# HGRN2 value projection by seven half-size products instead of eight, moved ahead of attention, its values kept in DRAM

## The chip, the cores and the metric

One core of one Trainium2 chip runs the whole program. The metric is the device time of one execution in microseconds (us). A time of a kernel is the median of several runs; the trace is one further execution taken by the hardware profiler. The engines are TensorE (PE, with its weight loads as PEld), VectorE (DVE), ScalarE (ACT), GpSimd (POOL) and SyncE (SP), whose queue issues nearly all DMA transfers in this kernel.

## What is computed

A hybrid decoder layer on 512 tokens of width 2048. One projection of the normalised input feeds an attention group (16 heads, with compressed, selected and windowed keys and values) and an HGRN2 group (8 heads with a 128x128 state each). Cut to what matters here:

```python
h = rmsnorm(x, norm_in[l])                       # 512 x 2048
proj = h @ w_in[l]
(q_a, k_cmp, v_cmp, k_slc, v_slc, k_win, v_win, gate_a, z_a,
 q_h, f_h, i_h, z_h) = jnp.split(proj, split_at, axis=-1)
o_a = nsa_mixer(q_a, k_cmp, v_cmp, ...)          # attention, 16 heads
o_h = hgrn2_mixer(q_h, f_h, i_h, lbs[l])         # i_h: 512 x 1024, the values of HGRN2
...
x = rmsnorm(x + concat(o_a, o_h, gated) @ w_out[l], final_norm)
```

The change concerns `i_h`, the product of h (512 x 2048) with 1024 columns of `w_in`.

## The kernel before

The normalised input is held transposed in SBUF as 16 tiles `hT[.][k]` of 128 features x 512 tokens, split in two parts: `hh` (rounded to fp32r) and `hl` (the rest). Weights come from DRAM in 512 KB pieces; ACT casts the rounded part (L281) and DVE subtracts for the rest (L282). Each product of a weight tile with an input tile is therefore three matmuls: rounded by rounded, rounded by rest, rest by rounded. A 128x512 matmul is one of those three.

The stages, in the order in which the driver at the end of the program calls them: the input is loaded, squared (ACT L201) and transposed while the compressed keys' projection runs (`first_proj(KC)`, L302 to L304); `x_norm` makes the row scales `rs` and `rs_bc` (DVE L209 and the small operations of `rsqrt`); the compressed values' projection VC (`proj_fm`, L323 to L325, 96 matmuls of 128x512) runs with nothing beside it but the cutting of the key blocks (`blocks(KC)`, SP copies from SBUF to SBUF, DVE L383); then VS (`proj_tm`, L348 to L350, 256 columns) beside the compression of the keys (`compress`, L399), VW and the first queries beside the compression of the values, and attention with further projections between its steps. After attention `hgrn_v(0)` computes four heads' values alone (192 matmuls of 128x512, ACT L832 scales the result by `rs`), and then four pairs of `hgrn_head` run (L730 and others), filled with projections: `hgrn_qf(1)`, `hgrn_v(1)` (192 matmuls more), `hgrn_qf(2)`, `hgrn_qf(3)` and the output gates. `FILL` says how much filling each pair of heads gets. Gates and the output projection end the program.

`run((generator, weight), ...)` interleaves generators by the costs they yield. Each engine carries out its own instructions strictly in one order, which a scheduler fixes at build time, and every DMA issue on SP is such an instruction too: one that waits holds up all those behind it. Buffers come from pools in which a slot is free again when its last reader is done.

## Time and profile before

| what | value |
|---|---|
| median of 3 runs (lowest to highest) | 1105.23 us (1104.85 to 1105.31) |
| the profiled execution: its own time, its span | 1106.74 us, 1104.7 us |
| granted TensorE clock, mean | 0.997 |
| TensorE matmuls busy | 1086.3 us, 98% of the span |
| VectorE, ScalarE, GpSimd busy | 572.0, 394.3, 76.1 us |
| DMA traffic | 109.60 MB, mean 99 GB/s |

The profiled execution is 2.0 us longer than its span (launch and end lie around it) and 1.5 us longer than the median. TensorE's busy time counts overlapping matmuls once; the mean duration of one matmul is longer than the distance between the starts of two, because they are pipelined. In rows of single instructions the time in front is the start from the span's beginning, the next the duration; what stands in brackets is the idle time ahead and what ended it.

### The profile page before, as it was taken

The numbers are of one execution on the slowest core, as the hardware profiler recorded it, in microseconds if no ns is written. First come the engines' busy times: TensorE is split into PE (matmuls) and PEld (weight loads), VectorE is DVE, ScalarE is ACT, GpSimd is POOL, SyncE is SP. The second block draws the span as 40 slices with busy tenths as digits, with TensorE's granted clock in tenths as the row PEclk, the third lists the DMA queues.
The fourth block names the chain that finished last, engine by engine and source line by source line (L and its number), as shares of the span: only waits on it lengthen the run. The fifth ranks groups of instructions, "written<-read, shape, count | busy, mean of one in ns | idle before, by whom it ended". The sixth has DMA issues, their size and how long they took to land.

```text
span 1104.7 us, 15078 instructions
## 1 busy us (share of the span) xinstructions
PE 1086.3 (98%) x5682; PEld 896.8 (81%) x5682; DVE 572.0 (52%) x1438; ACT 394.3 (36%) x798; POOL 76.1 (7%) x134
## 2 busy tenths in 40 slices
...
GB/s 256 122 142 191 115 145 104 71 83 58 115 59 57 76 39 39 96 77 96 77 77 61 92 78 80 82 81 73 76 130 81 95 115 115 126 112 173 96 86 124
DMA packets 91751, 109.60 MB, mean 99 GB/s; under 512 B 5584, under 2 KB 60448, under 8 KB 91680
## 3 DMA queue, kind: packets, MB, share of 16 engines
...
## 4 chain that ended last, share of the span: by engine, by line
PE 94%; DMA 2%; ACT 1%; DVE 1%; issue 1%; SPq 0%; ACTq 0%
PE pj L348 13%; PE pj L349 13%; PE pj L350 13%; PE pj L323 10%; PE pj L325 10%; PE pj L324 10%; PE ot L581 4%; PE pj L562 3%; PE lp L730 3%; DMA w<-in_w_in_dram 2%; PE lp L548 2%; PE lp L549 1%; PE pj L973 1%; PE pj L972 1%; PE pj L974 1%; PE lp L399 1%
## 5 line engine op out<-in xcount | busy, mean ns | idle before, releaser
L282 DVE TENSOR_TENSOR w<-w,w 128x1024 fp32r<-128x1024 f32 (+3 forms) x151 | 182.3, 1208 | 255.7 <-PE pj L349 87.1
L281 ACT CAST w<-w 128x1024 fp32r<-128x1024 f32 (+3 forms) x151 | 156.8, 1039 | 300.1 <-DMA w<-in_w_in_dram 188.7
L348 PE MATMUL pj<-w,hh 128*128 128x512 f32 (+2 forms) x608 | 229.1, 377 | 0.0
L349 PE MATMUL pj<-w,hl 128*128 128x512 f32 (+2 forms) x608 | 225.1, 370 | 0.0
L350 PE MATMUL pj<-w,hh 128*128 128x512 f32 (+2 forms) x608 | 224.5, 370 | 0.0
L323 PE MATMUL pj<-hh,w 128*128 128x512 f32 x480 | 194.8, 406 | 0.0
L325 PE MATMUL pj<-hh,w 128*128 128x512 f32 x480 | 189.1, 394 | 0.0
L324 PE MATMUL pj<-hl,w 128*128 128x512 f32 x480 | 188.9, 393 | 0.0
L350 PEld LDWEIGHTS pj<-w,hh 128*128 128x128 f32 x608 | 114.2, 188 | 18.8
L348 PEld LDWEIGHTS pj<-w,hh 128*128 128x128 f32 x608 | 114.5, 188 | 18.1 <-ACT s L486 0.4
L349 PEld LDWEIGHTS pj<-w,hl 128*128 128x128 f32 x608 | 114.5, 188 | 17.7
L325 PEld LDWEIGHTS pj<-hh,w 128*128 128x128 f32 x480 | 90.2, 188 | 19.4 <-issue 0.9
L324 PEld LDWEIGHTS pj<-hl,w 128*128 128x128 f32 x480 | 90.4, 188 | 16.9 <-issue 0.5
L323 PEld LDWEIGHTS pj<-hh,w 128*128 128x128 f32 x480 | 90.3, 188 | 16.9 <-issue 0.7
L522 ACT ACTIVATE s<-s,mn 128x128 f32<-128x128 f32 (+3 forms) x128 | 71.7, 561 | 41.6 <-DVE mn L517 36.5
L517 DVE CUSTOM_DVE_ANT_0 s<-s,lp 128x128 f32<-128x128 f32 (+3 forms) x128 | 60.3, 483 | 37.2 <-PE lp L549 18.5
L562 PE MATMUL pj<-ident,s 128*128 128x128 f32 x320 | 53.7, 275 | 0.7 <-ACT s L522 0.5
L581 PE MATMUL ot<-pt,s 128*64 128x512 f32 (+3 forms) x256 | 47.9, 441 | 1.4 <-ACT pt L571 1.4
L562 PEld LDWEIGHTS pj<-ident,s 128*128 128x128 f32 x320 | 39.5, 140 | 11.1 <-ACT s L522 4.7
L571 ACT COPY pt<-pj 128x256 f32<-128x256 f32 (+2 forms) x56 | 25.8, 461 | 48.0 <-PE pj L562 47.8
L581 PEld LDWEIGHTS ot<-pt,s 128*64 128x64 f32 x256 | 22.2, 136 | 23.5 <-issue 10.5
L348 PE MATMUL pj<-w,s 128*128 128x512 f32 x96 | 37.5, 391 | 0.0
...
## 6 DMA issues: line engine op xcount, KB each, us to landing
w<-in_w_in_dram SPq DMA_DIRECT2D x115, 512.0 KB, 3.6
w<-in_w_out_dram SPq DMA_DIRECT2D x32, 512.0 KB, 3.8
s<-s SPq DMA_DIRECT2D x56, 128.0 KB, 2.3
s<-in_x_dram SPq DMA_DIRECT2D x16, 256.0 KB, 6.5
l<-in_x_dram SPq DMA_DIRECT2D x12, 256.0 KB, 3.2
out_dram<-l SPq DMA_DIRECT2D x12, 256.0 KB, 2.7
...
w<-in_cmp_w_k_dram SPq DMA_DIRECT2D x4, 512.0 KB, 5.8
```

The source lines that it names most:

```text
L281: nc.scalar.copy(hi, raw)
L282: nc.vector.tensor_tensor(lo, raw, hi.bitcast(FP32), ALU.subtract)
L323: nc.tensor.matmul(acc[j], wh, hh, start=kk == 0, stop=False)
L324: nc.tensor.matmul(acc[j], wh, hl, start=False, stop=False)
L325: nc.tensor.matmul(acc[j], wl, hh, start=False, stop=kk == NK - 1)
L348: nc.tensor.matmul(o, ah, hi[:, k, :], start=kk == 0, stop=False)
L349: nc.tensor.matmul(o, al, hi[:, k, :], start=False, stop=False)
L350: nc.tensor.matmul(o, ah, lo[:, k, :], start=False, stop=kk == NK - 1)
L517: nc.vector.tensor_tensor_reduce(out=y, in0=e["bias"][:, 384 - i * P:512], in1=lp, scale=1.0, scalar=3e38, op0=ALU.add, op1=ALU.min, accum ...
L522: nc.scalar.activation(y, y, AF.Exp, bias=mn, scale=-1.0, accum_out=e["ls"][:, 2 * i + b:2 * i + b + 1])
L562: nc.tensor.transpose(tps[:, j * P:(j + 1) * P], y[:, j * P:(j + 1) * P], ident)
L581: nc.tensor.matmul(e["ot"][b * 64:(b + 1) * 64, j * P:512], v_tok[j][:, b * 256 + g * DH:b * 256 + (g + 1) * DH], e["pt"][:, b, j * 512:38 ...
```

## The change

The values `i_h` are a product of h, cut into 2 x 2 blocks, with the weights, cut into 2 x 2 blocks: eight half-size products before. `seven` computes them by seven products of sums and differences of blocks. With 48 matmuls of 128x512 for a half-size product, 336 matmuls take the place of 384. The blocks of h are called A11, A12, A21, A22 (A21 lies in the second half of the tokens of every even k), their sums S1 to S4; the blocks of the weights are combined while they are loaded (`first`, `second`, `third`), one j for each pair of k tiles, j = 0 to 7.

The new stage stands between VC and VS, with pools of its own (`s2`, `s14`, `u`, `e`) that are closed before the slabs and weight pools of the rest are opened. `second_proj` is the VC projection in eight steps of two k tiles (12 matmuls each); beside it `all_sums` makes S1 to S4 on DVE and ACT, one j a step. S3 is written over A21, which is copied to DRAM beforehand (8 transfers, `a21`) and brought back afterwards (8 transfers). `seven` runs three groups of products: (A11, S2, S3), (A12, A22), (S1, S4), whose results are added up by DVE, scaled by ACT and stored to DRAM (8 transfers of 256 KB, `v_scr`). `rows_back` reads four of them back after attention and four before the second pair of heads. The compressed keys' and values' projections go to DRAM as well (`keep`), and the copies of `blocks` read from there, after the new stage. The masks of attention are made after the new stage too. `hgrn_v` is gone, NLATE and FILL are changed. Rows of the changed kernel's order, below, carry its own line numbers.

```diff
-NLATE = 13
+NLATE = 18
-FILL = (62, 62.5, 62, 41)
+FILL = (51, 46, 45, 45)
+NU = 32
+NE = 10
...
+    def parts(src, shape=None):
+        hi, lo = [t if shape is None else t.rearrange(shape[0], **shape[1]) for t in (u(F32R), u(F32R))]
+        nc.scalar.copy(hi, src)
+        nc.vector.tensor_tensor(lo, src, hi.bitcast(FP32), ALU.subtract)
+        return hi, lo
...
+    def second_proj(acc):
+        acc += [pj(), pj()]
+        for k0 in range(0, NK, 2):
+            hi, lo = parts(load_u(w_in2, k0, C_VC), KC2)
+            for j in range(2):
+                js = slice(j * P, (j + 1) * P)
+                for k in range(2):
+                    hh, hl = hT[0][k0 + k], hT[1][k0 + k]
+                    nc.tensor.matmul(acc[j], hi[:, k, js], hh, start=k0 + k == 0, stop=False)
+                    nc.tensor.matmul(acc[j], hi[:, k, js], hl, start=False, stop=False)
+                    nc.tensor.matmul(acc[j], lo[:, k, js], hh, start=False, stop=k0 + k == NK - 1)
+            yield 2.7
...
+    def corner(q, part):
+        return hb[part][q][:, 0:4:2, 256:512].bitcast(FP32)
+    sums = {}
+    def sums_of(j):
+        (x0, y0), (x1, y1) = [[hT[part][k].bitcast(FP32) for part in range(2)] for k in (2 * j, 2 * j + 1)]
+        a0, a1, t = u(), u(), [u(), u()]
+        nc.vector.tensor_tensor(a0, x0, y0, ALU.add)
+        nc.vector.tensor_tensor(a1, x1, y1, ALU.add)
+        s3, s2, s1, s4 = t[0][:, 0:256], t[0][:, 256:512], t[1][:, 0:256], t[1][:, 256:512]
+        nc.vector.tensor_tensor(s3, a0[:, 256:512], a0[:, 0:256], ALU.subtract)
+        nc.vector.tensor_tensor(s1, a0[:, 256:512], a1[:, 256:512], ALU.add)
+        nc.vector.tensor_tensor(s2, a0[:, 0:256], s1, ALU.subtract)
+        nc.vector.tensor_tensor(s4, a1[:, 0:256], s2, ALU.add)
+        d2 = [space["s2"].tile([P, 256], F32R, name=nm("s2"), tag=f"s2_{part}{j}", bufs=1) for part in range(2)]
+        d14 = [space["s14"].tile([P, 512], F32R, name=nm("s14"), tag=f"s14_{part}{j}", bufs=1) for part in range(2)]
+        d3 = [hT[part][2 * j][:, 256:512] for part in range(2)]
+        sums[j] = {"S2": d2, "S1": [d[:, 0:256] for d in d14], "S4": [d[:, 256:512] for d in d14], "S3": d3,
+                   "A11": [hT[part][2 * j][:, 0:256] for part in range(2)],
+                   "A12": [hT[part][2 * j + 1][:, 0:256] for part in range(2)],
+                   "A22": [hT[part][2 * j + 1][:, 256:512] for part in range(2)]}
+        for (hi, lo), src in ((d2, s2), (d3, s3), (d14, t[1])):
+            nc.scalar.copy(hi, src)
+            nc.vector.tensor_tensor(lo, src, hi.bitcast(FP32), ALU.subtract)
+    def all_sums():
+        for q in range(4):
+            for part in range(2):
+                nc.sync.dma_start(out=a21[part][q], in_=corner(q, part))
+            for j in (2 * q, 2 * q + 1):
+                sums_of(j)
+                yield 2.7
...
+    w_half = w_in2.rearrange("(j h p) c -> h p j c", h=2, p=P)
+    free_banks = [(pj, pj), (pj, pj), (ps_lp, ps_lp), (ps_tp, ps_ot)]
+    def seven(c0, done):
+        def load(h, j, right):
+            raw = u()
+            nc.sync.dma_start(out=raw, in_=w_half[h][:, j, c0 + 512 * right:c0 + 512 * right + 512])
+            return raw
+        def group(products, prepare):
+            banks = [free_banks.pop(0) for _ in products]
+            accs = [[f() for f in b] for b in banks]
+            for j0 in range(0, 8, 2):
+                ops = [prepare(j) for j in (j0, j0 + 1)]
+                for i, name in enumerate(products):
+                    for tt in range(2):
+                        ts = slice(tt * P, (tt + 1) * P)
+                        for j in (j0, j0 + 1):
+                            ah, al = [a[:, ts] for a in sums[j][name]]
+                            hi, lo = ops[j - j0][i]
+                            nc.tensor.matmul(accs[i][tt], ah, hi, start=j == 0, stop=False)
+                            nc.tensor.matmul(accs[i][tt], al, hi, start=False, stop=False)
+                            nc.tensor.matmul(accs[i][tt], ah, lo, start=False, stop=j == 7)
+            free_banks.extend(banks)
+            return accs
+        t2 = [None] * 8
+        def first(j):
+            b22, b12, b11 = load(1, j, 1), load(0, j, 1), load(0, j, 0)
+            nc.vector.tensor_tensor(b12, b12, b22, ALU.subtract)
+            t2[j] = u()
+            nc.vector.tensor_tensor(t2[j], b12, b11, ALU.subtract)
+            return parts(b11), parts(t2[j]), parts(b12)
+        def second(j):
+            b21, t4 = load(1, j, 0), u()
+            nc.vector.tensor_tensor(t4, t2[j], b21, ALU.add)
+            return parts(b21), parts(t4)
+        def third(j):
+            b22 = load(1, j, 1)
+            nc.vector.tensor_tensor(t2[j], t2[j], b22, ALU.add)
+            return parts(t2[j]), parts(b22)
+        add = lambda out, a, b: nc.vector.tensor_tensor(out, a, b, ALU.add)
+        p1, p6, p7 = group(("A11", "S2", "S3"), first)
+        c11, u2, u3, c21 = [[ev(), ev()] for _ in range(4)]
+        for tt in range(2):
+            nc.scalar.copy(c11[tt], p1[tt])
+        for tt in range(2):
+            add(u2[tt], p6[tt], c11[tt])
+        for tt in range(2):
+            add(u3[tt], p7[tt], u2[tt])
+        p2, p4 = group(("A12", "A22"), second)
+        for tt in range(2):
+            add(c11[tt], p2[tt], c11[tt])
+            done(0, tt, c11[tt])
+        for tt in range(2):
+            add(c21[tt], p4[tt], u3[tt])
+            done(0, 2 + tt, c21[tt])
+        p5, p3 = group(("S1", "S4"), third)
+        for tt in range(2):
+            add(u3[tt], p5[tt], u3[tt])
+            add(u2[tt], p5[tt], u2[tt])
+            done(1, 2 + tt, u3[tt])
+        for tt in range(2):
+            add(u2[tt], p3[tt], u2[tt])
+            done(1, tt, u2[tt])
...
+    def v_done(half, t, y):
+        nc.scalar.mul(y, y, rs[:, 0, t:t + 1])
+        nc.sync.dma_start(out=v_scr[half][t], in_=y)
...
+    def keep(acc):
+        fs = [dram(), dram()]
+        for j in range(2):
+            f = ev()
+            nc.vector.tensor_tensor(f, acc[j], rs_bc, ALU.mult)
+            nc.sync.dma_start(out=fs[j], in_=f)
+        return fs
...
-    def hgrn_v(c):
-        hv[c] = [late() for _ in range(NT)]
-        def done(t, acc):
-            nc.scalar.mul(hv[c][t], acc, rs[:, 0, t:t + 1])
-        yield from proj_tm([], w_in2, hT, C_IH + c * 512, 512, done)
+    def rows_back(scr_, alloc):
+        tiles = [alloc() for _ in range(NT)]
+        for t in range(NT):
+            nc.sync.dma_start(out=tiles[t], in_=scr_[t])
+        return tiles
...
-    kblk = blocks(KC, 32)
-    run((proj_fm(VC, C_VC, 256), 1))
+    kf = keep(KC)
+    run((second_proj(VC), 22), (all_sums(), 22))
+    vf = keep(VC)
+    seven(C_IH, v_done)
+    first_part.close()
+    slabs = ctx.enter_context(ExitStack())
+    for name in ("w", "slab"):
+        space[name] = slabs.enter_context(tc.tile_pool(name=name, bufs=1))
+    att = ExitStack()
+    space["att"] = att.enter_context(tc.tile_pool(name="att", bufs=1))
+    for q in range(4):
+        for part in range(2):
+            nc.sync.dma_start(out=corner(q, part), in_=a21[part][q])
+    kblk = blocks(kf, 32)
...
-    run((hgrn_v(0), 41))
+    hv[0] = rows_back(v_scr[0], late)
     sz = [[] for _ in range(4)]
-    fill = chain(hgrn_qf(1), hgrn_v(1), hgrn_qf(2), hgrn_qf(3), z_proj(C_ZA, sz[0]), z_proj(C_ZA + 512, sz[1]))
+    fill = chain(hgrn_qf(1), hgrn_qf(2), hgrn_qf(3), z_proj(C_ZA, sz[0]), z_proj(C_ZA + 512, sz[1]))
     for c, t in enumerate(FILL):
+        if c == 1:
+            hv[1] = rows_back(v_scr[1], late)
```

Where the change moves instructions, at three places. **VectorE during the VC projection.** Before, what stands there is the end of the row scales, the weight subtractions (L282), two multiplications of the KC result from the PSUM tiles `pj` (L367) and the cutting of the key blocks (L383):

```order
L211 TENSOR_SCALAR rs<-rs 128x4 [waits DVE_49]
L282 TENSOR_TENSOR w_577<-w_574,w_576 128x1024 [waits DMAHW2_49,Activation_49]
L367 TENSOR_TENSOR s_502<-pj_191,rs_bc 128x512 [waits DMAHW6_49,Activation_49]
L367 TENSOR_TENSOR s_510<-pj_192,rs_bc 128x512 [waits DMAHW0_49]
L282 TENSOR_TENSOR w_607<-w_604,w_606 128x1024 [waits DMAHW3_49,Activation_49]
L383 TENSOR_TENSOR s_518<-s_504,col 128x4x31 [waits DMAHW5_49,DMAHW4_49]
```

Now one step of `second_proj` with `all_sums` reads as follows (j = 3; `u_641` and `u_642` are the two parts of a VC weight chunk, the `s_` tiles the parts of S2 and of S1 with S4, `hh_28` and `hl_29` the input tiles of a quad, in whose A21 corner S3 is written):

```order
L315 TENSOR_TENSOR u_642<-u_639,u_641 128x512 [waits DMAHW3_49,DMAHW2_49,Activation_49]
L372 TENSOR_TENSOR u_657<-hh_28_148,hl_29_149 128x512 [waits DMAHW5_49]
L373 TENSOR_TENSOR u_658<-hh_28_148,hl_29_149 128x512 [waits DMAHW6_49]
L375 TENSOR_TENSOR u_659<-u_657 128x256 [waits DVE_49]
L376 TENSOR_TENSOR u_660<-u_657,u_658 128x256 [waits DVE_49]
L377 TENSOR_TENSOR u_659<-u_657,u_660 128x256 [waits DVE_49]
L388 TENSOR_TENSOR hl_29_149<-u_659,hh_28_148 128x256 [waits Activation_49]
L378 TENSOR_TENSOR u_660<-u_658,u_659 128x256 [waits DVE_49]
L388 TENSOR_TENSOR s_165_668<-u_659,s_164_667 128x256 [waits Activation_49]
L388 TENSOR_TENSOR s_167_670<-u_660,s_166_669 128x512 [waits Activation_49]
L315 TENSOR_TENSOR u_680<-u_677,u_679 128x512 [waits DMAHW4_49,Activation_49]
```

Eight such steps stand one behind the other, and the last row is the first of the next step: 10 operations a step, of 512 and of 256 columns, and the VC chunk's subtraction (L315) of a step stands behind all the sums of the step before. Three subtractions (L388) wait for casts on ACT. The same 8 steps, with 4 multiplications (L537) and 27 small operations, fill all of DVE's rows from `rs`'s first (L232, before L209) to the first of `seven` (L429).

**SyncE during the first group of products.** The `u_` tiles are weights for `first` (three loads a j); the L1101 rows bring the A21 corner of the first quad back from DRAM, and wait for the products with S3 of j = 0 and 1:

```order
L405 DMA u_925<-in_w_in_dram 128x512 [waits DMAHW0_49,PE_49]
L405 DMA u_927<-in_w_in_dram 128x512 [waits DMAHW1_49]
L405 DMA u_929<-in_w_in_dram 128x512 [waits DMAHW2_49]
L1101 DMA hl_27_147<-d_163 128x2x256 [waits DMAHW3_49,PE_49]
L1101 DMA hh_26_146<-d_159 128x2x256 [waits DMAHW4_49,PE_49]
L405 DMA u_946<-in_w_in_dram 128x512 [waits DMAHW5_49,Activation_49]
L405 DMA u_948<-in_w_in_dram 128x512 [waits DMAHW6_49,DVE_49]
L405 DMA u_950<-in_w_in_dram 128x512 [waits DMAHW7_49,DVE_49]
L405 DMA u_1003<-in_w_in_dram 128x512 [waits DMAHW0_49,DVE_49]
```

Nothing stood here before. The three loads for j = 3 come behind the two returns; the pattern comes again ahead of the loads for j = 5 and for j = 7 and once ahead of the second group's load for j = 1.

**SyncE at the beginning of VS.** Before, VS's first weights (`w_634`, `w_668`) and the first compression weights were issued behind the key block copies while VC ran:

```order
L145 DMA w_634<-in_w_in_dram 128x4x256 [waits DMAHW4_49,Activation_49]
L395 DMA s_688<-in_cmp_w_k_dram 128x2x64 [waits DMAHW5_49]
L395 DMA s_688<-in_cmp_w_k_dram 128x2x64 [waits DMAHW6_49]
L145 DMA w_668<-in_w_in_dram 128x4x256 [waits DMAHW7_49,PE_49]
L390 DMA w_686<-in_cmp_w_k_dram 128x4x256 [waits DMAHW0_49,PE_49,Activation_49]
L390 DMA w_725<-in_cmp_w_k_dram 128x4x256 [waits DMAHW1_49,PE_49]
L145 DMA w_747<-in_w_in_dram 128x4x256 [waits DMAHW2_49,DVE_49,PE_49]
```

Now the stores of the values (L474) stand among the loads. The first row is the last of four stores, ahead of the third group's load for j = 1; then come the store of the third group's first finished product, VS's first weights `w_1688`, three stores, a compression weight, the eight key block reads from DRAM (the first of them shown), and VS's second weights `w_1767`:

```order
L474 DMA d_170<-e_1166 128x512 [waits Activation_49]
L405 DMA u_1396<-in_w_in_dram 128x512 [waits DMAHW7_49,DVE_49,PE_49]
...
L474 DMA d_173<-e_1163 128x512 [waits DMAHW6_49,Activation_49]
L160 DMA w_1688<-in_w_in_dram 128x4x256 [waits DMAHW7_49,PE_49]
L474 DMA d_174<-e_1164 128x512 [waits DMAHW0_49,Activation_49]
L474 DMA d_171<-e_1161 128x512 [waits DMAHW1_49,Activation_49]
L474 DMA d_172<-e_1162 128x512 [waits DMAHW2_49,Activation_49]
L568 DMA w_1706<-in_cmp_w_k_dram 128x4x256 [waits DMAHW3_49]
L547 DMA s_1603<-d_511 64x512 [waits DMAHW4_49,DMAHW2_49,DMAHW5_49,DMAHW1_49,DMAHW6_49,DMAHW0_49,DVE_49]
...
L568 DMA w_1745<-in_cmp_w_k_dram 128x4x256 [waits DMAHW4_49]
L160 DMA w_1767<-in_w_in_dram 128x4x256 [waits DMAHW5_49]
```

VS's first weights now stand behind a store that waits for a finished product of the third group, the key block reads behind the last stores, and VS's second weights behind those reads.

## Rows read from the trace of the kernel before

**Rows 1.** The page, part 1: busy us, share of the span, instructions.

```profile
PE 1086.3 (98%) x5682; PEld 896.8 (81%) x5682; DVE 572.0 (52%) x1438; ACT 394.3 (36%) x798; POOL 76.1 (7%) x134
```

**Rows 2.** The page, part 4: the chain that ended last, by engine.

```profile
PE 94%; DMA 2%; ACT 1%; DVE 1%; issue 1%; SPq 0%; ACTq 0%
```

**Rows 3.** PE by time, end of VC: start us, duration us, instruction.

```profile
61.02 0.39 PE L325 MATMUL pj<-hh,w 128*128 128x512 f32 x1
61.25 0.28 PE L348 MATMUL pj<-w,hh 128*128 128x256 f32 x1
61.37 0.28 PE L349 MATMUL pj<-w,hl 128*128 128x256 f32 x1
```

**Rows 4.** VC's stretch: busy PE, PEld, DVE, ACT, POOL; clock, DMA share, GB/s.

```profile
38.50:61.25 22.75, 22.59 (x101) 18.44 (x101) 13.19 (x44) 5.56 (x7) 0.00 (x0) 1.00 0.67 189
```

**Rows 5.** DVE in order of time, beginning of VC, as in rows 3.

```profile
36.29 0.17 DVE L209 TENSOR_REDUCE ss<-ss_in 128x4 f32<-128x20 f32 x1 [3.91 <-ACT s L201]
...
39.87 0.16 DVE L130 TENSOR_TENSOR rxt<-rxi 128x4 f32<-128x4 f32 x1
...
40.58 0.16 DVE L133 TENSOR_TENSOR rxi<-rxi,rxt 128x4 f32<-128x4 f32 x1
```

**Rows 6.** DVE in order of time, an attention step with 512 columns.

```profile
283.67 0.69 DVE L446 TENSOR_TENSOR s<-s,s 128x512 fp32r<-128x512 f32 x1 [2.54 <-ACT s L445]
284.28 0.55 DVE L517 CUSTOM_DVE_ANT_0 s<-s,lp 128x384 f32<-128x384 f32 x1
```

**Rows 7.** ACT in order of time, the cast ahead of that subtraction.

```profile
283.02 0.61 ACT L445 CAST s<-s 128x512 fp32r<-128x512 f32 x1
```

**Rows 8.** DVE in order of time, 256 columns in an HGRN2 head.

```profile
784.31 0.42 DVE L714 TENSOR_TENSOR s<-s,s 128x256 f32<-128x256 f32 x1
784.64 0.42 DVE L709 TENSOR_TENSOR s<-s,s 128x256 f32<-128x256 f32 x1
```

**Rows 9.** DVE in order of time, PSUM multiplications and block cutting.

```profile
42.31 1.29 DVE L367 TENSOR_TENSOR s<-pj,rs_bc 128x512 f32<-128x512 f32 x2
...
49.82 2.29 DVE L383 TENSOR_TENSOR s<-s,col 128x124 f32<-128x124 f32 x8 [0.52 <-DMA s<-s]
```

**Rows 10.** An issue on SP's queue: start us, duration us, transfer.

```profile
48.96 0.53 SPq L145 DMA_DIRECT2D w<-in_w_in_dram  x1
```

**Rows 11.** DMA issues: transfer, queue, count, KB each, median us to landing.

```profile
w<-in_w_in_dram SPq DMA_DIRECT2D x115, 512.0 KB, 3.6
...
s<-s SPq DMA_DIRECT2D x56, 128.0 KB, 2.3
s<-in_x_dram SPq DMA_DIRECT2D x16, 256.0 KB, 6.5
l<-in_x_dram SPq DMA_DIRECT2D x12, 256.0 KB, 3.2
```

**Rows 12.** The end of the program by stretch, columns as in rows 4.

```profile
1097.00:1098.00 1.00, 0.00 (x0) 0.00 (x0) 0.85 (x5) 0.00 (x0) 0.00 (x0) 0.92 0.00 0
1098.00:1099.00 1.00, 0.00 (x0) 0.00 (x0) 0.94 (x3) 0.78 (x2) 0.00 (x0) 0.50 0.00 0
```

**Rows 13.** PE in order of time, the first work of the program.

```profile
5.81 1.12 PE L192 MATMUL lp<-ident,w 128*128 128x128 f32 x4 [3.04 <-DMA w<-in_x_dram]
...
9.51 0.63 PE L302 MATMUL pj<-hh,w 128*128 128x512 f32 x1
9.94 0.63 PE L303 MATMUL pj<-hl,w 128*128 128x512 f32 x1
...
12.68 0.40 PE L303 MATMUL pj<-hl,w 128*128 128x512 f32 x1
12.92 0.39 PE L304 MATMUL pj<-hh,w 128*128 128x512 f32 x1
```

**Rows 14.** DVE in order of time, preparing the first heads after attention.

```profile
456.40 0.69 DVE L851 TENSOR_TENSOR s<-pj,rs_bc 128x512 f32<-128x512 f32 x1
...
458.74 0.43 DVE L709 TENSOR_TENSOR s<-s,s 128x256 f32<-128x256 f32 x1 [0.19 <-POOL s L745]
```

149 lines of the change are left out of this document (89 added, 60 removed).

## The prediction, made before the change was run

> **What bounds the kernel now.** I read the page's busy line and chain first: TensorE is busy 98% of the span [rows 1] and makes up 94% of the chain that ended last [rows 2]. What TensorE is relieved of is therefore gained, and what it is made to wait for is lost, nearly in full. VectorE's 52% [rows 1] is an average; the change puts its work in one place, so the stage counts. In VC's stretch (38.50 to 61.25) TensorE is busy 22.59 of 22.75 us, VectorE 13.19, ScalarE 5.56 [rows 4]. After it the next matmul, VS's first, follows at 0.23 us, the spacing of VC's own 128x512 matmuls; 256 columns take 0.12 [rows 3]. I price matmuls by these start distances, not by the mean duration (0.39 us in the same rows), which overlaps.
>
> **The change part by part.** The sum is made against the profiled execution's own 1106.7 us, 1.5 above the median.
>
> *A, matmuls removed.* 384 less 336 is 48, by 0.23 us: **-11.0**.
>
> *B, the sums.* Beside VC, VectorE gets ten operations a step where TensorE has 12 matmuls, 12 x 0.23 = 2.8 us. Prices: a 512-column subtraction starts 0.61 us ahead of its successor and lasts 0.69 itself [rows 6]; with 256 columns 0.33 and 0.42 [rows 8]. A step is three 512-column operations (the chunk's subtraction L315 and two additions), 3 x 0.61 = 1.83; four additions of 256 columns, 1.32, plus 0.1 because L377 needs L376's end; two subtractions of 256, 0.66; and the S1/S4 subtraction, 0.61. That last one waits for a cast of 512 columns on ScalarE, 0.61 [rows 7], which can only begin when L378 has ended, 0.42 after its start, and only one 256-column operation lies beside: 0.42 + 0.61 + about 0.08 for the two handovers, less 0.66, is 0.45. Together 5.0 us against TensorE's 2.8. The bounds are 4.4 (starts only, no wait) and 5.7 (durations throughout, with the wait). VectorE begins at 36.3 (its reduction of the squares) and has 8 steps, 40.0; 27 small operations that stay, 0.10 each by the seven starts from 39.87 to 40.58 [rows 5], 2.7; four multiplications out of PSUM at 0.65 [rows 9], 2.6; then the first three operations of the new stage, 1.9. So the third matmul of group 1 starts at 83.5, the two ahead of it 0.46 earlier, at 83.0 where VS began at 61.25: **+21.8** (17 to 27.5). VectorE then waits for no more than that one cast a step; TensorE is the one that waits, before each chunk's third matmul.
>
> *C, returns ahead of loads.* In group 1 the loads of j = 3, 5, 7 are queued on SP behind two returns that wait for the end of the pair before. From there: two returns and two loads issued, 4 x 0.53 [rows 10], the third load (the one whose product comes first) landing 3.2 later (256 KB, [rows 11]), a cast of 0.61: 5.9 us, while TensorE has the 18 matmuls of the even j, 4.1. Three times 1.8: **+5.4**. Bounds: 0 if landing is as quick as the smallest row here (2.3 us, 128 KB) and the returns start a little early, three times 5.1 with the 6.5 us that such a load took in company [rows 11].
>
> *D, group 1 to 2.* The same with one load: 2 x 0.53 + 3.2 + 0.61 = 4.9 against 12 matmuls of j = 0, 2.8: **+2.1** (0 to 5.4).
>
> *E, group 2 to 3.* The load of j = 1 stands behind four stores. From the group's last matmul: four additions on VectorE, 2.4, the last scaling on ScalarE 0.65, the store's issue 0.53, the load 3.2, its addition 0.69, its cast 0.61: 8.1. TensorE has only j = 0 in between, 2.8, which itself begins 3.7 late (the four additions, its own addition and its cast): **+5.3** (3 to 9).
>
> *F, group 3 to VS.* VS's first weights are issued behind the store of the first finished product. That product's last matmul lies 9 matmuls, 2.1 us, ahead of the group's end T; addition 0.69, scaling 0.61, issue 0.53 bring it to T - 0.3; the 512 KB land 3.6 later [rows 11]; the cast, two times 512 columns, 1.2: VS starts at T + 4.5, and its fifth matmul needs the subtraction, 1.2 more, against 0.6 of work ahead: +5.1. Next late are the key blocks: the last store is issued at T + 2.1, the eight reads wait for its landing (about T + 5), 8 x 0.53 of issue, 2.3 to landing, a cut of 2.29 / 8 [rows 9]: T + 11.5, when VS's 48 matmuls (0.12 each) run out at about T + 11. The second compression weight and VS's second weights are issued behind those reads and come 0.5 to 1 us late each: +2. Together **+7.1** (3 to 13). Before, all of this ran under VC. The masks now made by GpSimd ahead of the blocks' last columns end inside this wait.
>
> *G, the clock.* The granted clock is 1.00 in VC's stretch [rows 4]; at the program's end, with no matmul after 1095.2, it is 0.92 in the stretch from 1097 and 0.50 (1.2 GHz) from 1098 [rows 12]. The idle times of E and F (3.7 before group 3 begins, 4.5 before VS) are as long. I put 2 us for slow restarts (0 to 13, below). The Trainium skill, "TensorE: Matmul & The Clock Gate", section "Why this matters for your kernels", warns of gaps between bursts of matmuls, after which the clock is back at half. By that rule the half-idle VC stage and each start of a group would be slow, and the sum would come to the time of the third rival; this trace agrees only as far as its end shows the drop, since no burst follows there.
>
> *H, the heads.* Before, 192 matmuls lie between attention and the first head; now only 13 follow the second head's gate values, 3.0 us. That head's preparation takes 2.8 (456.40 to 459.17, [rows 14]): just covered, **0** (-1 to +4). The reads of V (3.2 us each) go out before the heads and are hidden by their first levels; without that cover they would cost some 3 us, inside these bounds. Smaller fillings take matmuls away from the heads, but no VectorE work is added.
>
> Sum: -11.0 + 21.8 + 5.4 + 2.1 + 5.3 + 7.1 + 2 = +32.7, or 1139.4 for such an execution, 1.5 less for the median: **1138**.
>
> **The rivals.**
> 1. *Only the sums stand in the way.* C to F shrink to their lower ends, about 6 in all, because transfers land earlier on a queue that moves little else. Then 1105.2 - 11.0 + 21.8 + 6 = 1122. For it: a 128 KB transfer lands in 2.3 us. Against: the waits for results, not landings, make most of E and F.
> 2. *Slow restarts.* The stage with gaps drops TensorE to 1.2 GHz. At the program's start matmuls came 0.43 apart (9.51 to 9.94) and 0.24 from 12.68 on [rows 13]; from 5.81 to about 12.4 it worked at the slow rate, so that half of 6.6, 3.3 us, was lost. Four such starts (three groups and VS) cost 13.2, and in VC 12 x 0.43 = 5.2 against 5.0 a step costs 1.6 more; less G's 2: 1151. The granted clock in the records of those stretches would decide.
> 3. *Faster: the sums hide.* If a VectorE step took less than 3.6 us, group 1 would begin less than 11 us late, at 72; with C to F at nothing the whole gains. At 2.8 a step it begins at 36.3 + 22.4 + 2.7 + 2.6 + 1.9 - 0.46 = 65.4, and the time is 1105.2 - 11.0 + 4.2 = 1098. Against it: starts alone give 4.4 a step.
> 4. *No net change*: a step near 3.6, as just said, or heads that gain what the stage loses. No row speaks for either.
>
> **How the numbers follow.** Forecast 0.60, as likely as the ten operations' prices and the order of the queue are sure. Its own range is 1128 to 1150: B's bounds, with half of the widths of C to F. Rival 1 has 0.17 and rival 2 0.17; rival 3 has 0.03 and no net change 0.03. The range that is to hold the time 8 times in 10 reaches over rivals 1 and 2: below, 17 for B and 8 for C to F give 1119; above, rival 2 with some 6 of late landings gives 1157. What a measurement here can tell from no change is 0.2%, 2.2 us: faster 0.03, same 0.03, slower 0.94.
>
> **What would show it.** In the changed kernel's trace: VectorE busy nearly without a break from 36 to 83, with TensorE at about half in that stretch, waiting for VectorE at the VC lines; the first matmul of `seven` near 83; in group 1 three waits of some 2 us for loads, with SP's returns just ahead; some 4 us idle ahead of group 3 and ahead of VS, with stores among the loads; 48 matmuls fewer. A and the heads are right if everything after VS has the same length but for 384 matmuls less. The forecast fails if VectorE's operations overlap more than these rows show, if SP's queue is not what holds the loads, or if the clock falls in the gaps.

## The result, and the profile after

| kernel | median of the runs (lowest to highest) | ratio to before, 95% interval |
|---|---|---|
| before | 1105.04 us (1104.44 to 1105.31) | |
| changed | 1170.45 us (1167.69 to 1171.13) | 1.0588 [1.0570, 1.0606] |

The change costs 65 us. The direction was foreseen, the size was not: 33 were predicted, and the result lies 13 us above the wider range (1119 to 1157). The changed kernel's page, its busy line and its chain by engine (before: [rows 1, 2]):

```profile
PE 1109.2 (95%) x5634; PEld 897.7 (77%) x5634; DVE 649.5 (56%) x1603; ACT 420.9 (36%) x871; POOL 73.6 (6%) x134
PE 86%; DMA 5%; DVE 3%; ACT 2%; SPq 1%; issue 1%; ACTq 0%; DVEq 0%
```

TensorE has 48 instructions fewer, yet is busy 23 us longer: part of the loss is in the matmuls, not in waits. What TensorE waited for (line and tile, releaser: us in total, times, longest):

```profile
PE pj L419 <- ACT u L314: 20.2, 7, 4.1
PE pj L354 <- ACT u L314: 11.7, 7, 2.6
PE pj L520 <- ACT w L307: 5.8, 1, 5.8
...
PE lp L577 <- POOL s L287: 1.6, 1, 1.6
```

The second row is VC beside the sums, the first the seven products, the third VS's first matmul, the fourth the compression of the keys, which waits for the masks. The waits and their causes follow in order of time. VectorE's step of VC goes from one L315 to the next:

```profile
54.71 0.69 DVE L315 TENSOR_TENSOR u<-u,u 128x512 fp32r<-128x512 f32 x1
...
59.09 0.69 DVE L388 TENSOR_TENSOR s<-u,s 128x512 fp32r<-128x512 f32 x1 [0.35 <-ACT s L387]
59.70 0.69 DVE L315 TENSOR_TENSOR u<-u,u 128x512 fp32r<-128x512 f32 x1
```

Then come TensorE at the beginning of group 1, SP's queue and TensorE around the first return, the transition to group 3, and VS's first matmul with the SP rows ahead of it:

```profile
84.41 0.79 PE L419 MATMUL pj<-u,hh 128*128 128x512 f32 x1 [4.11 <-ACT u L314]
85.00 0.63 PE L420 MATMUL pj<-u,hl 128*128 128x512 f32 x1
85.43 0.63 PE L421 MATMUL pj<-u,hh 128*128 128x512 f32 x1
...
95.58 0.59 SPq L1101 DMA_DIRECT2D hl<-d  x1
96.27 0.56 SPq L1101 DMA_DIRECT2D hh<-d  x1
96.92 3.02 SPq L405 DMA_DIRECT2D u<-in_w_in_dram  x6
...
104.10 0.80 PE L419 MATMUL pj<-u,hh 128*128 128x512 f32 x1 [4.12 <-ACT u L314]
...
167.29 0.50 PE L419 MATMUL pj<-u,s 128*128 128x512 f32 x1 [2.27 <-ACT u L314]
171.56 0.50 PE L419 MATMUL pj<-u,s 128*128 128x512 f32 x1 [1.24 <-ACT u L314]
...
190.87 0.33 SPq L474 DMA_DIRECT2D d<-e  x1
191.28 0.39 SPq L160 DMA_DIRECT2D w<-in_w_in_dram  x1
196.77 0.58 PE L520 MATMUL pj<-w,hh 128*128 128x256 f32 x1 [5.83 <-ACT w L307]
```

These are stretches of the new stage (length; busy PE, PEld, DVE, ACT, POOL; then the granted clock, DMA share, GB/s; before: [rows 4]):

```profile
60.00:70.00 10.00, 8.23 (x23) 6.11 (x23) 7.38 (x16) 2.02 (x5) 0.00 (x0) 0.67 0.05 18
70.00:80.00 10.00, 6.46 (x27) 4.53 (x25) 9.00 (x20) 4.00 (x9) 0.00 (x0) 1.00 0.00 0
80.00:90.00 10.00, 5.89 (x15) 4.39 (x14) 8.95 (x17) 4.58 (x9) 0.00 (x0) 0.68 0.73 237
...
120.00:130.00 10.00, 9.83 (x34) 7.48 (x32) 3.75 (x6) 1.47 (x3) 0.00 (x0) 0.77 0.27 81
```

The reader is to see two more things here. First, the granted clock, 1.00 in VC before, drops in VC and after most of the long idle times, and the matmuls of 85.00 and 85.43 start 0.43 apart, at 1.2 GHz. Second, there is a loss that no wait shows. These are the matmuls of one line of the projections by operands (duration min/median/max in ns), two rows of after and one of before:

```profile
L522 PE MATMUL pj<-w,hh x480: 277/394/582, 198.0 to 1114.6; 128*128 128x512 f32 x117, 128*128 128x256 f32 x22, 128*128 128x304 f32 x21
L522 PE MATMUL pj<-w,s x96: 387/389/397, 980.6 to 1092.1; 128*128 128x512 f32 x96
L350 PE MATMUL pj<-w,hh x608: 278/389/529, 61.5 to 1050.6; 128*128 128x512 f32 x120, 128*128 128x256 f32 x16, 128*128 128x304 f32 x16
```

In after, the moving operand of the first row lies in the pool `big` (`hh`), that of the second in a slab tile (`s`): the median is 394 ns against 389. (The rows with `hh` hold some matmuls of 256 and 304 columns too; most have 512, and the median is one of these.) Before, it was 389 for both. The starts say it better. The first two rows are the ends of a run of 14 matmuls at full clock at the end of group 2 of after, 0.234 us apart; the last two are the ends of a run of eight before, 0.227 apart:

```profile
161.58 0.39 PE L420 MATMUL pj<-u,hl 128*128 128x512 f32 x1
164.62 0.40 PE L421 MATMUL pj<-u,hh 128*128 128x512 f32 x1
...
999.84 0.39 PE L348 MATMUL pj<-w,hh 128*128 128x512 f32 x1
1001.43 0.39 PE L349 MATMUL pj<-w,hl 128*128 128x512 f32 x1
```

In group 3 of the same trace, whose two operands lie in `u` and `s14`, the distance is 0.227 again (176.04 to 190.55). In the built kernel before, `big`, which holds the weights too, and the slabs begin at 64 bytes past a multiple of 256. The changed kernel no longer keeps that: `big` is at 64, but `small`, which the allocator has put behind it, moves `u`, `w`, `s2`, `s14` and the slabs to 224. Counted over the two built programs, 16 of the 3472 matmuls of 128x512 before have operands that begin at different places modulo 256; now 2944 of 3424 have, 2928 of them 160 bytes apart.

### The profile page after: what moved, and what is told of

Read it like the earlier page. It is cut to its first block, busy times and chain, and to the rows that moved or that the text cites. A ratio compares the mean times of both kernels' runs of the same rounds, so it can differ in the third digit from the quotient of the medians.

```text
span 1169.4 us, 15419 instructions
## 1 busy us (share of the span) xinstructions
PE 1109.2 (95%) x5634; PEld 897.7 (77%) x5634; DVE 649.5 (56%) x1603; ACT 420.9 (36%) x871; POOL 73.6 (6%) x134
## 4 chain that ended last, share of the span: by engine, by line
PE 86%; DMA 5%; DVE 3%; ACT 2%; SPq 1%; issue 1%; ACTq 0%; DVEq 0%
PE pj L520 10%; PE pj L522 10%; PE pj L521 10%; PE pj L495 9%; PE pj L497 9%; PE pj L496 8%; PE ot L758 4%; PE pj L739 3%; PE lp L907 3%; DMA w<-in_w_in_dram 2%; DMA u<-in_w_in_dram 2%; PE lp L725 2%; PE lp L726 1%; PE pj L1167 1%; PE pj L1168 1%; PE pj L1169 1%
## 5 line engine op out<-in xcount | busy, mean ns | idle before, releaser
L308 DVE TENSOR_TENSOR w<-w,w 128x1024 fp32r<-128x1024 f32 (+1 forms) x126 | 152.8, 1214 | 189.1 <-ACT w L307 62.5
L307 ACT CAST w<-w 128x1024 fp32r<-128x1024 f32 (+1 forms) x126 | 130.9, 1040 | 234.0 <-DMA w<-in_w_in_dram 153.5
L520 PE MATMUL pj<-w,hh 128*128 128x512 f32 (+2 forms) x480 | 181.3, 378 | 5.8 <-ACT w L307 5.8
L495 PE MATMUL pj<-hh,w 128*128 128x512 f32 x448 | 184.8, 413 | 0.0
L497 PE MATMUL pj<-hh,w 128*128 128x512 f32 x448 | 178.4, 398 | 0.0
L521 PE MATMUL pj<-w,hl 128*128 128x512 f32 (+2 forms) x480 | 178.2, 372 | 0.0
L522 PE MATMUL pj<-w,hh 128*128 128x512 f32 (+2 forms) x480 | 177.7, 372 | 0.1
L520 PEld LDWEIGHTS pj<-w,hh 128*128 128x128 f32 x480 | 91.8, 191 | 21.1 <-ACT w L307 6.4
L522 PEld LDWEIGHTS pj<-w,hh 128*128 128x128 f32 x480 | 91.3, 191 | 16.2 <-DVE w L308 0.3
L521 PEld LDWEIGHTS pj<-w,hl 128*128 128x128 f32 x480 | 91.9, 191 | 14.8
L497 PEld LDWEIGHTS pj<-hh,w 128*128 128x128 f32 x448 | 84.2, 188 | 20.2 <-issue 1.0
L495 PEld LDWEIGHTS pj<-hh,w 128*128 128x128 f32 x448 | 84.3, 188 | 16.9 <-issue 0.7
L314 ACT CAST u<-u 128x512 fp32r<-128x512 f32 x72 | 42.1, 619 | 65.1 <-DMA u<-in_w_in_dram 38.4
L315 DVE TENSOR_TENSOR u<-u,u 128x512 fp32r<-128x512 f32 x72 | 47.9, 688 | 14.0 <-ACT u L314 12.6
```

Of the source, the lines that this page charges most:

```text
L307: nc.scalar.copy(hi, raw)
L308: nc.vector.tensor_tensor(lo, raw, hi.bitcast(FP32), ALU.subtract)
L495: nc.tensor.matmul(acc[j], wh, hh, start=kk == 0, stop=False)
L497: nc.tensor.matmul(acc[j], wl, hh, start=False, stop=kk == NK - 1)
L520: nc.tensor.matmul(o, ah, hi[:, k, :], start=kk == 0, stop=False)
L521: nc.tensor.matmul(o, al, hi[:, k, :], start=False, stop=False)
```

## The experiments

Each time is a median in us, followed by its ratio to runs of the kernel before on the same chip (1106.2 to 1106.4 us) with the 95% interval. "After" is the changed kernel. It was timed on another chip, on which the kernel before took 1105.0, so differences of medians to it are uncertain by some 1.3 us.

### Where the operands lie

The theory is that the distance of two matmuls depends on where their operands begin in SBUF. The rival is that the longer distance comes with the new work beside it.

```diff
a_pad    -            a, pre = sm(3, "la"), sm(1, "lp")
         +            a, pre = sm(3, "la"), sm(1, "lp", bufs=1)
b_shift  (the kernel before, the same edit, and a tile ahead of hT)
         +    big.tile([P, 8], FP32, name="pad", tag="pad", bufs=1)
a_align       small = ctx.enter_context(tc.tile_pool(name="small", bufs=2))
         +    big = ctx.enter_context(tc.tile_pool(name="big", bufs=1))
         (big opened behind small, no longer ahead of it)
```

> The changed kernel with 4 bytes a partition fewer in a small pool, so that the pools behind it (s2, w, s14, u, slab) begin 32 bytes earlier, at a multiple of 64 as the input tiles hh and hl do; no instruction differs but one small buffer that is no longer doubled. Theory A (operand placement: a matmul whose two operands differ by 32 modulo 64 bytes starts 7 ns later): the spacing of 128x512 matmuls falls from 0.234 to 0.227 us throughout, and the time from 1170 to about 1152 to 1156. Theory B (the whole chip or the profile was slower, placement does nothing): same time within 2 us, spacing unchanged.

Measured: 1168.6, 1.0562 [1.0542, 1.0582], a miss: a common multiple of 64 is not what counts. The pools move by 32 bytes, so that the operands differ by 128 modulo 256. The same 14 matmuls (161.41 to 164.43) are 0.232 apart, the median duration is 392 ns: between the two others. The time is within the spread of after.

> The kernel before with a 32-byte gap between the weight buffers w and the input tiles hh and hl (slab moves along with hh); nothing else. Theory A (placement): spacing of the weight matmuls goes from 0.227 to 0.234 us, and the time from 1105 to between 1117 and 1129. Theory B: 1105 within 2 us.

Measured: 1122.4, 1.0144 [1.0129, 1.0159]. This is the kernel before with 32 bytes more in front of its input tiles and no other work; it is 16 us slower. The slabs move with the input tiles, the weights do not, so that both of these rows are slow:

```profile
L351 PE MATMUL pj<-w,hh x608: 277/395/532, 61.1 to 1064.4; 128*128 128x512 f32 x120, 128*128 128x256 f32 x16, 128*128 128x304 f32 x16
L351 PE MATMUL pj<-w,s x96: 390/396/399, 928.5 to 1042.0; 128*128 128x512 f32 x96
```

> The changed kernel with the two lines swapped that open the pools big (input tiles) and small, so that every pool read by TensorE begins at the same place modulo 256 bytes as the input tiles (224; in the changed kernel the input tiles lie at 64 and the rest at 224, in the kernel before all at 64); no instruction differs. The 4-byte-fewer run put the difference at 128 modulo 256 and left the spacing at 0.2325. Theory A (a 128x512 matmul starts 6 to 8 ns later unless its operands agree modulo 256): spacing 0.227 throughout, time 1170 less 15 to 20, 1150 to 1156. Theory B (the spacing has another cause): 1168 to 1172.

Measured: 1158.0, 1.0464 [1.0444, 1.0484], 12.4 us less than after (somewhat less than the 15 to 20 expected), with the order of two lines exchanged:

```profile
L522 PE MATMUL pj<-w,hh x480: 278/389/582, 194.8 to 1101.6; 128*128 128x512 f32 x117, 128*128 128x256 f32 x22, 128*128 128x304 f32 x21
```

The theory stands: the distance was 0.227 us at equal remainders modulo 256, 0.232 at a difference of 128, 0.233 to 0.234 at odd multiples of 32. The rival falls with b_shift, which has no new work, and with a_align, which has all of it.

### The returns on SP's queue (step C)

```diff
-            nc.sync.dma_start(out=corner(q, part), in_=a21[part][q])
+            nc.gpsimd.dma_start(out=corner(q, part), in_=a21[part][q])
```

> The changed kernel with the eight returns of the A21 corners issued from GpSimd's queue in place of SP's. Theory A (the loads of j = 3, 5, 7 are late because the returns ahead of them on SP wait for a pair's end): the three waits of 4.1 us in group 1 shrink to under 1 us, with them some slow restarts, and the time falls by 12 to 18 us, to 1152 to 1158. Theory B (the loads wait for buffer slots or for the DMA engines): the waits stay above 3 us and the time within 4 us of 1170.

Measured: 1151.2, 1.0407 [1.0389, 1.0424], 19.3 us less. Of the waits inside and behind group 1 (4.12, 4.08, 3.93, then 0.45 and 1.54) one of 0.45 is left, 13.7 us less. The clock is 0.99 to 1.00 in every stretch from 90 to 140, where after has 0.77 to 0.98; the rest of the gain, some 6 us, is put down to it. Step C's place is right; its price, 5.4, was less than half of the three waits, 12.1.

> Two edits to the changed kernel at once: all operands of the 512-column matmuls at one remainder of 256 (the order of two pools exchanged), and the sums' copies back on GpSimd's queue instead of SyncE's. If the two causes are separate, their gains add: alone they gave about 12 us and 19 us, so 1170 - 31 = about 1139 us, with an even spacing of 0.227 us and no wait of 4 us in group 1. If the copies' gain came partly from the same time as the placement's, the sum is smaller: 1143 to 1148 us.

Measured: 1139.8, 1.0305 [1.0291, 1.0319]. The two gains add up within 1 us. This is what TensorE still waits for:

```profile
PE pj L354 <- ACT u L314: 11.8, 7, 2.6
PE pj L419 <- ACT u L314: 7.0, 3, 4.2
PE pj L520 <- ACT w L307: 5.7, 1, 5.7
```

### The clock (step G against the second rival)

```diff
+    def keep_busy(a, b, n):
+        bank = ps_ot()
+        for i in range(n):
+            nc.tensor.matmul(bank, a, b, start=i == 0, stop=i == n - 1)
...
+            keep_busy(lo[:, 1, 0:P], hT[0][k0 + 1], 8)
...
+                if len(products) == 3 and j0:
+                    keep_busy(sums[j0]["S3"][0][:, 0:P], ops[0][2][1], 9)
```

> The changed kernel with matmuls added whose results nobody reads: 8 of 128x512 after each of the eight steps beside VC, and 9 ahead of the first product of j = 3, 5, 7 in group 1, where TensorE stood idle (64 + 27, 20 us of TensorE). Theory A (the idle gaps bring the clock down, and the slow matmuls after them cost some 11 us in the new stage and 2 us in the sums): granted clock 1.00 until group 1's end, group 1 begins 2 us earlier, matmuls 0.23 apart right after the gaps, the time 6 to 12 us shorter although work was added, about 1160. Theory B (the clock costs nothing, since the stage is bound by VectorE and loads): no shorter, 1168 to 1176.

Measured: 1165.5, 1.0534 [1.0515, 1.0553]. Some 20 us of matmuls whose result is not used were added, and the time fell by some 5, a little less than expected. Two of its stretches show the clock at 1.00, where after has 0.67 and 0.68:

```profile
60.00:70.00 10.00, 9.88 (x41) 7.35 (x40) 9.22 (x21) 3.93 (x9) 0.00 (x0) 1.00 0.17 52
80.00:90.00 10.00, 7.68 (x33) 5.94 (x32) 9.10 (x16) 4.48 (x8) 0.00 (x0) 1.00 0.70 221
```

Group 1 also begins at 82.70 in place of 84.41. In after, at the low clock, VC's matmuls had read S3's corner so late that the cast into it, and with it two of VectorE's steps, waited (1.30 and 1.17 us); here neither step waits for that.

### The sums (step B)

```diff
-        nc.vector.tensor_tensor(a0, x0, y0, ALU.add)
-        nc.vector.tensor_tensor(a1, x1, y1, ALU.add)
+        nc.gpsimd.tensor_tensor(a0, x0, y0, ALU.add)
+        nc.gpsimd.tensor_tensor(a1, x1, y1, ALU.add)
```

> The changed kernel with the first two additions of each j of the sums (512 columns) on GpSimd in place of VectorE. Theory A (group 1 is late by VectorE's 5.0 us a step against TensorE's 2.8): VectorE's step is 3.8 us, group 1 begins some 9 us earlier, at 75, and the time falls by 8 to 12 us, to about 1160. Theory B (GpSimd's additions are slow, or slow VectorE down by the port they share, and the step is bound by them): group 1 begins no earlier than 82, time 1168 or more.

Measured: 1169.7, 1.0574 [1.0557, 1.0592], the same as after. Group 1 begins at 80.40, 4 us earlier, and the last matmul of the compressions lies 4.6 earlier; by the end of the trace 1.9 of it is left. Where the rest went was not followed. VectorE and GpSimd in VC, first with GpSimd's additions beside, then without:

```profile
57.40 0.69 DVE L315 TENSOR_TENSOR u<-u,u 128x512 fp32r<-128x512 f32 x1
58.00 1.52 DVE L375 TENSOR_TENSOR u<-u 128x256 f32<-128x256 f32 x1
59.44 1.51 DVE L376 TENSOR_TENSOR u<-u,u 128x256 f32<-128x256 f32 x1
60.98 0.42 DVE L377 TENSOR_TENSOR u<-u,u 128x256 f32<-128x256 f32 x1
63.31 0.68 DVE L315 TENSOR_TENSOR u<-u,u 128x512 fp32r<-128x512 f32 x1
...
57.56 1.67 POOL L372 TENSOR_TENSOR u<-hh,hl 128x512 f32<-128x512 f32 x1 [2.81 <-DVE s L388]
59.19 1.47 POOL L373 TENSOR_TENSOR u<-hh,hl 128x512 f32<-128x512 f32 x1
...
68.59 0.68 DVE L315 TENSOR_TENSOR u<-u,u 128x512 fp32r<-128x512 f32 x1
72.55 0.69 DVE L315 TENSOR_TENSOR u<-u,u 128x512 fp32r<-128x512 f32 x1
```

The steps are of two kinds. While GpSimd works beside, a step takes VectorE 5.9 us, more than the 5.0 of after. GpSimd's last addition ends at 60.66, and from 68.59 on a step takes 3.96, near the 3.8 expected; TensorE's bursts in VC then follow one another at the same 3.96. So VectorE's sums do set the pace of VC. An addition of 256 columns takes VectorE 1.52 us beside one of GpSimd's and 0.42 alone. The Trainium skill, "SBUF — State Buffer", section "Who interferes with whom", says that a VectorE instruction with two SBUF inputs contends with a GpSimd instruction that reads SBUF; these rows agree.

```diff
(a_nosum: sums_of without its additions, subtractions and casts; all_sums and the driver without copies)
+        d2 = [hT[part][2 * j + 1][:, 0:256] for part in range(2)]
+        d14 = [hT[part][2 * j + 1] for part in range(2)]
```

> The changed kernel without the sums: S1 to S4 are not computed (the products read blocks of the input in their place), A21 is neither copied out nor brought back; everything else, the seven products too, as it was. Theory A (of the 65 us lost, the sums cost 23 by VectorE, the returns 12 by SP's queue, and the clock some 10 through both): group 1 begins near 62, its waits are gone, and the time is 1170 less 38 to 45, 1125 to 1132. Theory B (the loads of the products or the slots would hold group 1 anyway): 1140 or more.

Measured: 1141.3, 1.0316 [1.0301, 1.0332], 29 us less, where more was expected. The waits of group 1 are gone, but the order of SP's queue has changed with it: VS's weights are now behind the eight key block reads, and VS waits for 16.2 us (waits by line):

```profile
PE pj L507 <- ACT w L307: 16.2, 1, 16.2
```

SP's queue there:

```profile
161.11 0.60 SPq L537 DMA_DIRECT2D s<-d  x1
161.75 0.59 SPq L160 DMA_DIRECT2D w<-in_w_in_dram  x1
```

So this run puts the price of the sums with their copies at 29 us or more; it does not say how much more.

### Stores ahead of loads (steps E and F)

```diff
-        nc.sync.dma_start(out=v_scr[half][t], in_=y)
+        nc.gpsimd.dma_start(out=v_scr[half][t], in_=y)      (a_sto)
+        nc.scalar.dma_start(out=v_scr[half][t], in_=y)      (a_sto2)
```

> The changed kernel with the eight stores of the values issued from GpSimd's queue in place of SP's. Theory A (the third group's loads and VS's weights are late because they stand behind stores on SP): the waits of 2.3 and 1.2 us in group 3 fall to about 1 together, the 5.8 us ahead of VS to under 3, the time by 5 to 8 us, to 1162 to 1165. Theory B (the additions on VectorE and the shared buffers hold them, not the queue): within 2 us of 1170.

Measured: 1176.2, 1.0631 [1.0616, 1.0647]: 6 us more than after, a miss. VS begins at 191.81, 5 us earlier (E's second wait of 1.24 is among what is gone), but its own wait is 5.5 as before, and the masks, which GpSimd now makes behind its stores, hold the compression for 5.4 us instead of 1.65.

> The changed kernel with the stores of v on ScalarE's queue instead of SyncE's, so that neither the loads behind them (steps E and F) nor GpSimd's masks stand behind a store. If steps E and F are waits of a load queued behind a store, VS's matmuls begin about 5 us earlier (near 191.8, as with the stores on GpSimd's queue), nothing new waits for the masks, and the time is 1163 to 1166 us. If ScalarE's casts wait for the stores instead (they now share its order), the gain is lost: 1168 to 1173 us.

Measured: 1174.9, 1.0627 [1.0609, 1.0645], 4 us more than after, a miss. No store stands ahead of VS's weights any more, and the wait is the same. These are TensorE's last product, SP's load and VS's first matmul:

```profile
188.49 0.39 PE L421 MATMUL lp<-u,s 128*128 128x512 f32 x1
188.90 0.38 SPq L160 DMA_DIRECT2D w<-in_w_in_dram  x1
194.61 0.58 PE L520 MATMUL pj<-w,hh 128*128 128x256 f32 x1 [5.74 <-ACT w L307]
```

The load goes out 0.4 us after the last product's last matmul begins: it waits for the pools of the new stage, in whose memory the weight pool lies, not for a store. Ahead of group 3 one wait of 3.32 stands where after has two, 2.27 and 1.24, so that step E costs nearly the same with the stores on another queue. VS begins 2.2 us earlier; that and 4 us more are lost behind it, 2.2 of them in a longer wait for the masks (3.89 for 1.65). The rest was not found.

```diff
(d_w0: c_ret, and)
+    w0 = ctx.enter_context(tc.tile_pool(name="w0", bufs=1))    # 3 of the weight ring's 10 tiles, open all along
...
+        p2, p4 = group(("A12", "A22"), second, {4: lambda: vs_w.append(load_raw(w_in2, 0, 4, C_VS, 256))})
+        p5, p3 = group(("S1", "S4"), third, {6: lambda: vs_w.append(load_w(w_in2, 0, 4, C_VS, 256, raw=vs_w[0]))})
-NU = 32
-NE = 10
+NU = 28
+NE = 8
```

> The changed kernel with one remainder of 256 for the operands and the copies back on GpSimd's queue (1139.8 us), and now VS's first weights in three tiles of a pool of their own that was open all along, loaded during group 2 and split during group 3 (6 fewer tiles are left for the loads of the seven products). If the wait before VS is for the memory that the closed pools free after the last of the seven products, VS's matmuls follow the last product within 1 us and the time falls by about 5 us, to 1134 to 1136 us. If the wait is for the queue or the transfer itself, it stays or moves behind VS's first 48 matmuls: 1139 to 1141 us. Fewer tiles for loads may cost a wait in group 1, which the trace will show.

Measured: 1150.7, 1.0405 [1.0387, 1.0422]: 11 us more than c_ret, a miss in the time. In the trace VS's first matmuls, whose weights have memory of their own, now follow the last product at once or lie among the products. VS's second weights lie in the weight pool, and TensorE waits for them instead:

```profile
180.01 0.39 PE L426 MATMUL lp<-u,s 128*128 128x512 f32 x1
180.24 0.34 PE L527 MATMUL pj<-w,hh 128*128 128x256 f32 x1
...
194.30 0.58 PE L527 MATMUL pj<-w,hh 128*128 128x256 f32 x1 [10.97 <-ACT w L311]
```

The second weights go out on SP at 184.25, behind four stores and two compression weights, 4.2 us after the last product's last matmul begins, and their cast begins 8.95 later (193.20), so this wait is the queue's and the transfer's as well as the memory's. Nearly all of the loss lies in front: group 1 begins 11.5 us later than in c_ret (94.35 for 82.88). Of that, 7.8 is one wait at 26.68, a side effect: the scheduler moved the cast of VS's first weights into the program's head, where ScalarE waited 8.5 us for their transfer. It is in the next two runs as well, which are therefore compared with this one.

```diff
(d_nosum: d_w0 with the edit of a_nosum; d_warm: d_w0 with the first keep_busy of a_warm, in VC only)
```

> The run with VS's early weights, without the sums and the copies out and back (input blocks stand in for S1 to S4). If the prediction's step B is the largest cost that remains, VC's eight steps fall from 5.0 to about 2.8 us and the time by some 20 us, to 1112 to 1116 us; if the other waits of the seven products (D, E) and the lost clock vanish with it too, 1105 to 1110 us; if the sums were hidden by something else, less than 12 us is gained.

Measured: 1132.0, 1.0234 [1.0219, 1.0249]: 18.7 us less than d_w0. This run waits 12.3 us for the masks, which it reaches earlier, so that the sums cost 18.7 or more. That is near B's 21.8.

> The run with VS's early weights plus eight idle-time matmuls (128x512, their result is not used) in each of VC's eight steps, 14.5 us of added TensorE work where the sums bind. If the clock at the start of group 1 is lost because TensorE stands still beside the sums, the rows of 80 to 90 us are granted 1.00 instead of 0.66 and the time is 3 to 4 us less in spite of the added work; if the added work is paid for, it is up to 14 us more.

Measured: 1144.9, 1.0349 [1.0334, 1.0365]: 5.8 us less than d_w0, with 14.5 us of work added. The time is better than expected, the reason is not the one put: the stretch in which group 1 begins (90 to 100) has 0.83 in both runs, and group 1 begins only 1.45 us earlier (92.90 for 94.35). In VC it is 1.00, where d_w0 has 0.83 and 0.84 from 60 to 80. Another 1.2 us come in group 3, granted 1.00 where d_w0 has 0.83 (150 to 160), and 2.0 from a shorter wait for VS's second weights (8.96 for 10.97). Why the clock of group 3 should change with matmuls in VC these runs don't tell.

### VS beside VC

c_vs is c_ret with VS's 192 matmuls of 256 columns put into VC's eight steps (24 a step), its result kept in DRAM; the sums of a step follow two steps later. c_vs_sto has the stores of the values on ScalarE's queue as well.

```diff
+            for t in range(NT):
+                o = vs[t // 2][:, (t % 2) * 256:(t % 2) * 256 + 256]
...
+                    nc.tensor.matmul(o, ah, vh[:, k, :], start=kk == 0 and t % 2 == 0, stop=False)
+                    nc.tensor.matmul(o, al, vh[:, k, :], start=False, stop=False)
+                    nc.tensor.matmul(o, ah, vl[:, k, :], start=False, stop=kk == NK - 1 and t % 2 == 1)
+            if LAG <= j:
+                sums_of(j - LAG)
```

> The changed kernel with one remainder of 256 for the operands, the copies back on GpSimd's queue, and VS projected together with VC beside the sums, so that TensorE has 48 more small matmuls' worth of work (some 11 to 17 us) in each of the steps in which the sums now bind. If the prediction's reading of step B holds (the VectorE sums bind VC's eight steps, TensorE idles beside them), the work of VS costs nothing there: the time falls from 1139 us by the length of VS's own stage (10 to 13 us) and by its wait (5 us), to 1115 to 1128 us. If TensorE's clock or VectorE's order lengthens the steps in proportion, nothing is gained over 1139 us.

Measured: 1132.2, 1.0248 [1.0234, 1.0263], the fastest version that computes everything, 7.6 us below c_ret and 26 above the kernel before. The expected gain was 11 to 24. VC's stretch shows why it fell short:

```profile
37.00:88.00 51.00, 47.96 (x300) 42.57 (x298) 36.44 (x91) 17.66 (x36) 0.00 (x0) 1.00 0.30 94
```

With VS, TensorE is busy 47.96 of 51 us at full clock and no longer waits for VectorE: a step is now 12 x 0.23 + 24 x 0.12 = 5.6 us of matmuls against the sums' 5.0, so only the difference between TensorE's 2.8 and 5.0 was free. Group 1 begins 9.9 us later than in c_ret (92.80), after a wait of 6.9. The wait ends with a cast (ScalarE, 92.13) that waited for its load, and SP issued the loads of group 1 from 87.50 on, behind the stores of VS's own result (85.89): the pattern of step C once more. VectorE is busy with two steps' sums until 91.5, so that without the stores the group's third matmul would have come little earlier. The gain comes after the products, where VS's own stage is gone.

> As the run with VS beside VC, with the stores of v on ScalarE's queue too. If the waits of steps E and F are the queue's, 3 to 6 us less than that run, 1110 to 1124 us; if ScalarE's order takes their place, the same as that run. The kernel before (1105 us) is not expected to be beaten by over 1%: GpSimd, VectorE and the two DMA chains of the seven products are still there.

Measured: 1136.4, 1.0274 [1.0260, 1.0288], 4 us more than c_vs, as a_sto2 is 4 more than after: taking the stores off SP's queue gains nothing, and ScalarE's queue is a worse place for them.

## Why the prediction was right in direction and too small

Here is each step against the trace of after, in us:

| step | predicted | measured | read from |
|---|---|---|---|
| A | -11.0 | -10.9 | 48 x 0.227 |
| B | +21.8 | +23.2 | 84.41 less 61.25 |
| C | +5.4 | +12.1 | 4.12 + 4.08 + 3.93 |
| D | +2.1 | +2.0 | 0.45 + 1.54 |
| E | +5.3 | +3.5 | 2.27 + 1.24 |
| F, VS's weights | +5.1 | +5.8 | wait at 196.77 |
| G, and the operands' place, up to VS | +2 | +12.7 | 196.77 - 84.41 = 112.4, less 336 x 0.2267 and the 23.5 of C to F |
| F, what is late next, and all behind VS | +2 | +16.4 | 1159.77 - 196.77 (last matmul) against 1094.88 - 61.25 less 384 x 0.2267 |

The column adds up to 64.8; the last matmuls of the two traces lie 64.9 apart (1159.77 and 1094.88), the medians 65.4.

**B** was right: 4.99 us a step (54.71 to 59.70) for 5.0, a cast waited for 0.35, group 1 at 84.41 for 83.0. Behind the 1.4 us more, some terms cancel: VectorE begins 0.8 later (37.12), the two steps that the low clock lengthened cost 2.6, and the first steps with the small operations take 2 less than reckoned. The matmul at 84.41 itself was released by a load (ScalarE's cast at 83.74 waited for it); VectorE's third operation of the group ends at 85.08, so that the third matmul, at 85.43, could not have come much earlier.

**C is the first step that failed, as a size.** Place, queue and count were right; 5.4 was put, and 12.1 measured. The loads were priced at 3.2 us to landing, from transfers that mostly went out alone [rows 11]; issued six in a row behind two returns, their median was 5.5. From the first return's issue (95.58) to the end of the cast (104.05) it took 8.5 us where 5.9 was put. The upper bound of the step, three times 5.1, from the 6.5 us row in company, was nearer the truth than the value taken.

**G is the second, also as a size.** 2 us was put for slow restarts. In a_align, whose operands agree, the table's row for G is free of the operands' place and still comes to 10.5 (110.8 from group 1 to VS, less 76.2 of matmuls and 24.2 of waits), so that slow matmuls cost some 10 us there. The second rival's mechanism is real. The clock is granted at 0.67 and 0.68 in stretches of the new stage, and matmuls come 0.43 apart at the start of group 1, behind the waits of C and in two steps of VC. Behind F the 256-column matmuls come 0.21 apart instead of 0.12. Behind E, where G had put a slow restart too, there is none: from 160 to 180, with the waits of 2.27 and 1.24, the clock is 1.00. That slow matmuls follow gaps between bursts is what the Trainium skill, "TensorE: Matmul & The Clock Gate", section "Why this matters for your kernels", warns of, and this trace agrees behind the waits of 3.9 to 5.8 us; in VC the clock fell behind waits of 2.65 and 1.92 us. (The prediction says that by this rule the time would be that of the third rival; it is the second rival that it describes.) a_warm gives 5 us of it back, net of 20 us of added work. C and G go together: with the returns on another queue, 14 us of waits went and some 6 us with the clock.

The second rival was priced at 1151. With 6.7 more for C and 12.4 for the operands' place it would have come to 1170, but that is partly luck: it put its slow starts at the three groups and VS, and they fell elsewhere. The forecast's own range was also drawn too narrow: B's bounds with half of the widths of C to F give 1126 to 1155, not 1128 to 1150. The result lies above both.

**The operands' place was in no step.** It is worth 12.4 us by a_align and is most of the last row of the table: behind VS, a_align takes 10.6 of the 16.4 us away. The prediction took 0.23 us for a matmul everywhere, from one row, and said that everything after VS would keep its length.

**E and F** have about the right size for partly wrong reasons. E's first wait (2.27) is the additions and scalings of group 2, as put. Its second (1.24) ends with a load that went out at 167.16, just behind the four stores, as put; but a_sto2, without stores on SP, waits as long in one piece, and in a_sto and c_ret the second wait is gone behind matmuls at the low clock, whether the stores are on SP or not. So no run shows what the stores alone cost there. F's wait is not the store's: without any store ahead (a_sto, a_sto2) it is as long, and the load goes out when the last product is done, as the load's own wait on PE in the order's row says. By the program this is the memory of the closed pools, and in d_w0 the first weights, which have memory of their own, are there in time. The masks, which were to end inside F, held the compression for another 1.65.

**D and H** held: D to 0.1 us; the heads (the first to the last matmul of L730, now L907) are some 2.5 us longer than before less the 192 matmuls moved, and 0.1 in a_align, so that this too is the operands' place.

What remains of c_ret, 33.6 us over the kernel before by the medians and 32.3 by the traces, is made up of -10.9 for A, 21.6 until group 1 (82.88 for 61.25), 8.5 of waits from there to VS (0.5, 2.3, 5.7), 5.9 of slow matmuls in between (90.6 from 82.88 to 173.44, less 76.2 and 8.5) and 7.1 behind VS. Seven products for eight save 11 us here, and VectorE's sums alone cost twice that. No version tried comes near the kernel before. It stays open why stores on ScalarE's queue cost 4 us, what the rest behind VS is (5.8 us in a_align), and why the operands' place modulo 256 matters inside the engine.
